# A gradient along rows: unequal shares of the first load among the DMA engines, returned in the last store

## The chip, the cores and the metric

The kernel runs on one core of one Trainium2 chip. The metric is the device time of one execution in microseconds (us), the median of several runs. The engines that matter here are VectorE (DVE), GpSimd (POOL), SyncE (SP), whose queue issues the DMAs, and the sixteen DMA engines behind the queues.

## The reference

```python
x = np.random.randn(8192, 8192).astype(np.float32)

def reference(x):
    return np.gradient(x, axis=1)
```

For each row, `out[j] = (x[j+1] - x[j-1]) / 2` inside, `out[0] = x[1] - x[0]` and `out[m-1] = x[m-1] - x[m-2]` at the two ends. 268 MB are read and 268 MB written.

## The kernel before, in words

The 8192 rows of 8192 columns are cut into `nsets = 32` tiles of 256 rows. Each of the 128 partitions holds `R = 2` whole neighbouring rows, 64 KB in one piece, both in the DRAM and in the on-chip memory; a tile is 8.39 MB. There are `NB = 3` slots; a slot is 64 columns wider than the tile (`SH`), so that the result, which is written over the input 64 columns further left, never overtakes what is still to be read.

For tile `i` the steps are:

- `load(i)`, line 60: one DMA on SP's queue into slot `i % 3`. From tile 3 on it waits for the store that used the slot before.
- Line 70, POOL: the four end differences per partition, kept in the tile `ends`. It waits for the load.
- Line 76, DVE: one custom operation that computes half the difference for all of the two rows. It waits for line 70.
- Line 87, a copy of `ends` into the four end columns, on POOL for some tiles, on DVE for the others (for the last two tiles on DVE).
- Line 89: one DMA on SP's queue that stores the tile. It waits for line 87.

SP's order is written out by hand: loads 0, 1, 2; stores 0, 1, 2; loads 3, 4, 5; stores 3, 4, 5; and so on to stores 27, 28, 29; loads 30, 31; stores 30, 31. An SP instruction that waits holds up those behind it. `chain` declares which earlier steps an instruction needs, and replaces the dependencies that would be found automatically.

Of the kernel before, what the change touches and what calls it, by code (L numbers as in the profile page):

```python
# [1 line left out]

# [4 lines left out]


@with_exitstack
def kernel(  # L10
    ctx: ExitStack,
    tc: tile.TileContext,
    x: bass.AP,
    out: bass.AP,
):

    nc = tc.nc
    P = nc.NUM_PARTITIONS
    n, m = x.shape
    R = 2
    NB = 3  # L30
    SH = 64
    W = R * m
    nsets = n // (P * R)
    f32 = x.dtype

    x_sets = x.rearrange("(s p t) m -> s p (t m)", p=P, t=R)
    out_sets = out.rearrange("(s p t) m -> s p (t m)", p=P, t=R)

    pool = ctx.enter_context(tc.tile_pool(name="pool", bufs=1))
    slots = [pool.tile([P, SH + W], f32, name=f"slot{k}", tag=f"slot{k}") for k in range(NB)]  # L40
    ends = pool.tile([P, nsets, R, 2], f32, name="ends", tag="ends")
    loads, stores = [], [None] * nsets
    in_front = {}

    def chain(i, ins, *needed):

        group, engine = f"slot{i % NB}", ins.ins.engine
        keep = [o.ins for o in needed]  # L50
        if in_front.get(engine, (None,))[0] == group:
            keep.append(in_front[engine][1])
        tc.declare_no_dep(ins.ins, group=group, keep=keep, reason="implied by the needed step")
        tc.add_to_no_dep_group(group, ins.ins)
        in_front[engine] = group, ins.ins
        return ins

    def load(i):
        b = slots[i % NB]
        ins = nc.sync.dma_start(out=b[:, SH : SH + W], in_=x_sets[i])  # L60
        loads.append(chain(i, ins, *([stores[i - NB]] if i >= NB else [])))

    with tc.manual_schedule():
        for i in range(NB):
            load(i)
        for i in range(nsets):
            b = slots[i % NB]
            xin = b[:, SH : SH + W].rearrange("p (t m) -> p t m", m=m)

            ins = nc.gpsimd.tensor_sub(  # L70
                out=ends[:, i, :, :],
                in0=xin[:, :, 1 : m : m - 2],
                in1=xin[:, :, 0 : m - 1 : m - 2],
            )
            at = [chain(i, ins, loads[i])]
            ins = nc.vector._custom_dve(  # L76
                dve_ops.TENSOR_TENSOR_REDUCE_SUB_MAX,
                out=b[:, 1 : W - 1],
                in0=b[:, SH + 2 : SH + W],
                in1=b[:, SH : SH + W - 2],  # L80
                s0=0.0,
                s1=0.5,
            )
            halved = chain(i, ins, *at)
            res = b[:, 0:W].rearrange("p (t m) -> p t m", m=m)
            placer = nc.gpsimd if i % 5 in (1, 3) and i < nsets - 2 else nc.vector
            ins = placer.tensor_copy(out=res[:, :, 0 : m : m - 1], in_=ends[:, i, :, :])  # L87
            placed = chain(i, ins, halved)
            ins = nc.sync.dma_start(out=out_sets[i], in_=b[:, 0:W])
            stores[i] = chain(i, ins, placed)  # L90
            if i % NB == NB - 1:
                for k in range(i + 1, min(i + 1 + NB, nsets)):
                    load(k)


# [1 line left out]
_INS = ['x']  # L97
_OUTS = [((8192, 8192), 'float32')]


# [23 lines left out]
```

## Time and profile before

| | |
|---|---|
| median of three runs | 1248.04 us (1247.85 to 1248.38) |
| the profiled execution: span from the first to the last instruction | 1245.7 us |
| DVE busy | 554.6 us, 45% |
| POOL busy | 8.8 us, 1% |
| DMA queue q1 (SP's): share of sixteen engines' span | 99.8% |
| mean rate | 431 GB/s |
| line 76, one operation | 17.22 us |
| load, issue to landing (median) | 58.0 us |
| store, issue to landing (median) | 40.4 us |

The profiled execution has no device time of its own beside its span; the span is set against the median, and the 2.3 us between them are what lies around the span. Busy times are of compute instructions alone; a DMA shows as its issue on an engine's queue, and by its packets. The profile's page gives the packets in sum, and the trace has a record of each: start, duration, size and queue, but not the DMA engine that moved it. "Idle before, releaser" in the rows of an instruction is what its engine waited for last.

### The profile page before, as it was taken

What the parts mean: (1) busy time and instruction counts of PE and PEld (TensorE: products, weight loads), DVE (VectorE), ACT (ScalarE), POOL (GpSimd) and SP (SyncE); (2) the same over time, 40 slices, a digit from 0 to 9 for tenths busy, and PEclk for the clock granted to TensorE, in tenths of its full rate; (3) what the DMA queues carried; (4) which work ended last, traced back from release to release, by engine and by line L of the source; (5) the groups of instructions that cost most, each with busy time, mean ns of one, the idle gap of its engine ahead of it and who ended that gap; (6) DMA issues with size and microseconds to landing.
All of it is one profiled execution on the core that took longest, in us unless ns stands there. A gap on an engine that the chain in (4) does not pass through costs nothing.

```text
span 1245.7 us, 237 instructions
## 1 busy us (share of the span) xinstructions
DVE 554.6 (45%) x52; POOL 8.8 (1%) x48
## 2 busy tenths in 40 slices
DVE  2850583069009702850582079009603840591083
POOL 0000000000000000000000000000000000000000
DMA  9999999999999999999999999999999999999999
GB/s 404 438 436 423 427 431 438 438 438 436 436 427 431 425 438 436 425 434 436 429 434 436 434 436 434 436 434 438 419 436 436 434 438 438 431 434 429 429 410 404
DMA packets 9217, 536.88 MB, mean 431 GB/s; under 512 B 1024, under 2 KB 1024, under 8 KB 1024
## 3 DMA queue, kind: packets, MB, share of 16 engines
q1 hardware_dynamic: 9216, 536.88, 99.8%
q14 instruction: 1, 0.01, 0.0%
HBM read 268.44 MB, written 268.44 MB: 431 GB/s over the span
## 4 chain that ended last, share of the span: by engine, by line
another core or an unknown queue 74%; DVE 18%; DMA 3%; issue 2%; POOL 1%; SPq 0%; POOLq 0%
DVE slot L76 18%; DMA slot<-in_x_dram 3%; POOL ends L70 0%; POOL slot L87 0%; SPq L60 0%; POOLq L119 0%; DVE slot L87 0%
## 5 line engine op out<-in xcount | busy, mean ns | idle before, releaser
L76 DVE CUSTOM_DVE_ANT_0 slot<-slot 128x16382 f32<-128x16382 f32 x32 | 551.2, 17224 | 668.7 <-POOL ends L70 668.7
L70 POOL TENSOR_TENSOR ends<-slot 128x4 f32<-128x4 f32 x32 | 6.3, 198 | 989.6 <-DMA slot<-in_x_dram 989.6
L87 POOL COPY slot<-ends 128x4 f32<-128x4 f32 x12 | 2.3, 190 | 207.9 <-DVE slot L76 207.9
L87 DVE COPY slot<-ends 128x4 f32<-128x4 f32 x20 | 3.4, 172 | 0.7
L108 POOL MEMSET const-bfloat16-1.0<- 128x1 bf16 x1 | 0.1, 101 | 0.0
L108 POOL MEMSET const-uint8-127<- 128x1 uint8 x1 | 0.1, 101 | 0.0
L108 POOL MEMSET const-float32-0.0<- 128x1 f32 x1 | 0.1, 98 | 0.2 <-issue 0.2
L108 POOL MEMSET const-float32-1.0<- 128x1 f32 x1 | 0.1, 98 | 0.0
## 6 DMA issues: line engine op xcount, KB each, us to landing
slot<-in_x_dram SPq DMA_DIRECT2D x32, 58.0
out_dram<-slot SPq DMA_DIRECT2D x32, 40.4
```

The lines of the kernel that those rows point to most:

```text
L70: ins = nc.gpsimd.tensor_sub(out=ends[:, i, :, :], in0=xin[:, :, 1 : m : m - 2], in1=xin[:, :, 0 : m - 1 : m - 2],)
L76: ins = nc.vector._custom_dve(dve_ops.TENSOR_TENSOR_REDUCE_SUB_MAX, out=b[:, 1 : W - 1], in0=b[:, SH + 2 : SH + W], in1=b[:, SH : SH + W - 2],
L87: ins = placer.tensor_copy(out=res[:, :, 0 : m : m - 1], in_=ends[:, i, :, :])
L108: nc = _bacc.Bacc("TRN2", target_bir_lowering=False, num_devices=1)
```

## The change

The first load and the last store are each cut into several DMAs; everything between is as before.

- The first load becomes four DMAs on SP's queue: columns 0 to 6143 of both rows of partitions 112 to 127; partitions 0 to 111 whole; and the remaining 2048 columns of both rows, once for 12 partitions (112 to 123) and once for 4 (124 to 127). Line 70 of tile 0 waits for all four.
- The last store is cut the same way, but its last columns go out as four DMAs of 4 partitions each on Pool's queue; the two large parts stay on SP's.
- Two small loads on Pool's queue (64 columns of both rows of a few partitions, into a tile `turns` that nothing reads) are added: one of 4 partitions after the first three loads, and one of 12 partitions between the third and the fourth of the small stores.

```diff
+    EVEN, CUT = P - 16, m - 2048
+
+    def parts_of(dram, i, sb, last):
+        whole = dram.rearrange("(s p t) m -> s p t m", p=P, t=R)[i]
+        rows = sb.rearrange("p (t m) -> p t m", m=m)
+        cuts = [(slice(EVEN, P), slice(0, CUT))]
+        first = EVEN
+        for k in last:
+            cuts.append((slice(first, first + k), slice(CUT, m)))
+            first += k
+        pairs = [(whole[p, :, c], rows[p, :, c]) for p, c in cuts]
+        pairs.insert(1, (dram.rearrange("(s p t) m -> s p (t m)", p=P, t=R)[i][0:EVEN], sb[0:EVEN]))
+        return pairs
...
+    turns = pool.tile([16, R, 64], f32, name="turns", tag="turns")
...
     def load(i):
-        b = slots[i % NB]
-        ins = nc.sync.dma_start(out=b[:, SH : SH + W], in_=x_sets[i])
-        loads.append(chain(i, ins, *([stores[i - NB]] if i >= NB else [])))
+        sb = slots[i % NB][:, SH : SH + W]
+        after = [stores[i - NB]] if i >= NB else []
+        parts = parts_of(x, i, sb, (12, 4)) if i == 0 else [(x_sets[i], sb)]
+        loads.append(
+            [chain(i, nc.sync.dma_start(out=to, in_=of), *after) for of, to in parts]
+        )
+
+    def pass_by(first, k):
+        rows = x.rearrange("(p t) m -> p t m", t=R)[first : first + k, :, 0:64]
+        nc.gpsimd.dma_start(out=turns[first : first + k], in_=rows)
...
         for i in range(NB):
             load(i)
+        pass_by(0, 4)
...
-            at = [chain(i, ins, loads[i])]
+            at = [chain(i, ins, *loads[i])]
...
+            if i == nsets - 1:
+                parts = parts_of(out, i, b[:, 0:W], (4, 4, 4, 4))
+                for k, (to, of) in enumerate(parts):
+                    queue = nc.sync if k < 2 else nc.gpsimd
+                    chain(i, queue.dma_start(out=to, in_=of), placed)
+                    if k == 4:
+                        pass_by(4, 12)
+                continue
             ins = nc.sync.dma_start(out=out_sets[i], in_=b[:, 0:W])
             stores[i] = chain(i, ins, placed)
```

## The prediction

> **What bounds the kernel now.** I read the page first, the engine rows beside the DMA rows.
>
> ```profile
> span 1245.7 us, 237 instructions
> DVE 554.6 (45%) x52; POOL 8.8 (1%) x48
> ...
> DMA packets 9217, 536.88 MB, mean 431 GB/s; under 512 B 1024, under 2 KB 1024, under 8 KB 1024
> ...
> q1 hardware_dynamic: 9216, 536.88, 99.8%
> ...
> slot<-in_x_dram SPq DMA_DIRECT2D x32, 58.0
> out_dram<-slot SPq DMA_DIRECT2D x32, 40.4
> ```
>
> VectorE works 45% of the span; the one DMA queue works 99.8% of it. 64 transfers of 8.39 MB made 8192 large packets and 1024 tiny ones: per transfer 128 rows of 64 KB and 16 end marks, so each transfer runs on sixteen DMA engines, eight rows on each. All bytes at 431 GB/s take 1245.7 us. No compute edit matters; what matters is bytes per engine, and time in which an engine has none. Next, the windows near the end (start:end, length, DVE and POOL busy, clock, DMA share, GB/s):
>
> ```profile
> 1200.00:1202.00 2.00, 2.00 (x1) 0.00 (x0) 1.00 1.06 459
> 1202.00:1204.00 2.00, 2.00 (x1) 0.00 (x0) 1.00 0.46 197
> 1204.00:1206.00 2.00, 0.56 (x2) 0.00 (x0) 1.00 1.23 524
> ```
>
> These put a packet in one slice, so they swing by a packet's length, but the dip to 0.46 is real. The timeline says why:
>
> ```profile
> 1186.93 0.20 POOL L70 TENSOR_TENSOR ends<-slot 128x4 f32<-128x4 f32 x1 [77.07 <-DMA slot<-in_x_dram]
> 1187.17 17.22 DVE L76 CUSTOM_DVE_ANT_0 slot<-slot 128x16382 f32<-128x16382 f32 x1 [59.84 <-POOL ends L70]
> ...
> 1204.62 19.69 SPq L89 DMA_DIRECT2D out_dram<-slot  x2
> 1206.28 0.20 POOL L70 TENSOR_TENSOR ends<-slot 128x4 f32<-128x4 f32 x1 [19.14 <-DMA slot<-in_x_dram]
> ...
> 1223.77 0.17 DVE L87 COPY slot<-ends 128x4 f32<-128x4 f32 x1
> ```
>
> Load 30 has landed on all engines at 1186.93, and store 30 is issued 17.69 us later, at 1204.62. Until then an engine has only load 31. The trace's packet records (start and length of each packet; I joined each to the one that starts where it ends, which gives sixteen engines) show the rest: a 64 KB packet takes 2.42 us; before store 30 the slowest engine is 2.3 us behind the fastest, and four engines lie 2.1 to 2.3 behind. The fastest finish load 31 near 1202.4 and stand idle until store 30's first packet at 1204.9; the slowest finishes at 1205.26. From there all have two stores, 16 packets, 38.7 us, and end between 1243.7 and 1243.9. So the end is set by when the slowest engine finishes load 30, then 19.5 us until store 30's first packet, then 38.7 us, then 1.8 us until the span ends. The profiled execution's 1245.7 us stands 2.3 below the median of 1248.04; I take that difference as unchanged and add my sum to the median.
>
> **The change, part by part.**
>
> *First load in four transfers.* It issues three more on SP, 0.42 us each (the rows of the first three issues: 0.38, 0.42, 0.42). The first, 16 partitions by 2 rows by 24 KB, is 0.79 MB and 1.8 us at 431 GB/s, so the next is queued before it ends: nothing on the path. Loads 1 and 2 are issued 1.3 us later behind 19 us of queued work: nothing. Without that queue the price would be 1.3 us. L70 of tile 0 waits for four transfers; on Pool nothing else is due before tile 1, store 0 is issued at 40.40 while its turn in the queue comes after load 2 lands (L70 at 62.44), so 20 us hide any delay there. More descriptors (24 KB and 8 KB instead of 64 KB) have no row; from 0 to 0.1 us, taken as 0.
>
> *Shares.* The last 2048 columns of 16 partitions, 256 KB, an even 16 KB per engine, move as 12 and 4 partitions. If a partition's two rows stay on one engine, four engines have two such pieces, eight one and four none: +16 KB, 0 and −16 KB. 16 KB on an engine is 262144 B over sixteen at 431 GB/s, 0.61 us. So from the first tile on, four engines run 0.61 us late and four 0.61 early, up to the last store. What that does to load 30 depends on which engine is slowest: between −0.61 (all four late ones in the early group; the fifth is 0.8 us ahead of them) and +0.61 (the slowest of all in the late group). The records name no engines; with four late engines of sixteen, one in the group that gets more is likely. I take +0.4. The Trainium skill, "DMA: Bandwidth & Descriptors", section "Why a DMA increments its semaphore by 16 and not by 1", says that such a transfer takes the lowest-numbered engines, so that 0 to 3 would be late and 12 to 15 early; no row here shows engine numbers, and the first load's packets starting one after another over 0.69 us is only a hint at an order.
>
> *Last store.* 16 partitions by 24 KB and the other 112 go out on SP; the 256 KB go as four transfers of 4 partitions on Pool's queue, with a small load of 12 partitions before the fourth. If Pool's queue takes the sixteen engines in turn, one for each partition, the first tile's small load uses the first four, three of the stores the next twelve, the load of 12 the first twelve again, and the fourth store the last four: 0, 16 and 32 KB. Those that had 16 KB less now have 16 KB more, and per engine the bytes of the whole run are even. But the time is not: all engines but the slowest start store 30 together at 1204.9, so the early group's head start has been spent waiting, and its 16 KB more end 0.61 us after the others. Against the slowest engine of before, which ended about 0.2 after most, that is +0.4. The late group ends 0.61 earlier, which helps nobody.
>
> *Pool's issues.* No row shows a DMA issued on Pool. The nearest is SP's issue, 0.34 us: five are 1.7 us after 1223.97, beside store 31's 19.4 us. They reach the end only if one takes more than about 3.5 us (five in 17.5). The first small load stands before L70 of tile 0 on Pool, which waits 22.27 us there. Bounds 0 and +1 (completion seen later, a second queue mixed in); I take +0.1, near the SP row. A page speaks against it: the same page, "Rules for kernel authors", calls transfers under 64 KB mostly overhead, and its fit of 2.0 us for each would make five 10 us, 8 more than the row, still inside store 31 and so 0 by either.
>
> *Switches from loads to stores.* Here the change can pay. The records show the packet at such a switch lengthened: at the first (57.4 us) all sixteen took 3.16 to 3.82 us, 1.1 more than 2.42; at the nine later ones the mean extra was 0.18, 0.07, 0.41, 0.62, 0.15, 0.12, 0.35, 0.00 and 0.06 us, and the slowest engine lost 2.6 in all. Spread among the engines was 0.6 us at the first switch, 2.0 by the fifth, 2.4 in the last, cheap ones. So a spread made on purpose might be cheaper from the start; but the two dearest later switches came at spreads of 1.25 and 1.8, which the change would pass through, and in them the late engines lost most (that feeds the lag). Bounds −2.6 (all later losses gone) and +1; I take −0.3, as the rows point both ways.
>
> *Sum:* 0.4 + 0.4 + 0.1 − 0.3 = +0.6 us: 1248.6. 0.2% is 2.5 us, about what a measurement of this kernel can tell from no change; the sum is well inside.
>
> **The rivals.**
>
> *Shares misplaced (slower).* The last store's four small transfers go to the same engines each time, or to those that were late. Place: the last 19 us. Four pieces on one group are 64 KB, 48 KB over even: 1.8 us on the end. With 0.6 from the first tile if those are the late ones, the extra 0.1, and 0.4 if the lag feeds itself at the switches, +2.9: 1250.9. It decides 0.2% from about 66 KB of surplus, or its time, on the last engine. For it: Pool's placing is not in this trace, and the two helper loads only matter if a rotating turn exists. Against: counted in turns of sixteen, the sizes 4, 4, 4, 4, 12, 4 end where they began, on the right four, whatever the order of speeds.
>
> *Staggered switches (faster).* The switch losses mostly vanish: −2.6 for the later ones, up to −1.0 for the first, +0.8 for shares as above or −0.2 if load 30 comes earlier by the full 0.61: −1.8 to −3.8, so 1244.2 to 1246.2. For it: the cheap late switches at wide spread. Against: the 0.62 at 1.8 us of spread, and the first switch's loss is also the first writing at all.
>
> *Nothing happens.* If the hardware spreads 12 and 4 partitions evenly, or the lagging engines are in the middle and the tail hides the rest, 1248.0 to 1248.2.
>
> **How the numbers follow.** Forecast 0.45, misplaced 0.27 (0.25 of it over 1250.5), staggered switches 0.20 (0.13 of it below 1245.5), nothing 0.08. The likeliest case alone spans −1.5 to +2.0, 1246.5 to 1250.0. To hold 8 in 10 I go to 1245.4 and 1251.2. Faster 0.13, within 0.2% 0.62 (0.45, 0.08, and the 0.09 that the two other cases leave inside), slower 0.25.
>
> **What would show it.** In the packet records, after tile 0 engines in groups 0.6 us apart; the L70 of tile 30 at 1186.9 plus or minus 0.6, store 30 issued 17.7 us behind it. Some engines' last packets 0.6 us behind the rest, Pool's small packets all gone before 1235. Wrong would be: tile 30's L70 more than 1.5 us early (switches cheaper than I took), Pool's packets among the last, a span end more than 1.8 us behind the last large packet, or one engine with four small pieces.

## The result, and the profile after

The changed kernel takes 1281.74 us (median of four, 1280.38 to 1282.05) against 1248.21 for the kernel before beside it: ratio 1.0267, interval 1.0254 to 1.0281, 33.5 us slower. The profiled execution's span is 1278.4 us against 1245.7. The page of the changed kernel, header, row 2, row 3 and the DMA issues (KB each, median us from issue to landing):

```profile
span 1278.4 us, 255 instructions
...
DMA  9999999999999999999999999999999999999997
GB/s 219 338 437 443 429 429 433 441 433 429 437 435 437 424 433 431 439 437 431 429 439 437 431 433 435 433 437 429 427 445 433 431 431 437 437 433 433 433 379 250
DMA packets 9585, 536.89 MB, mean 420 GB/s; under 512 B 1280, under 2 KB 1296, under 8 KB 1296
...
slot<-in_x_dram SPq DMA_DIRECT2D x1, 768.0 KB, 10.1
out_dram<-slot SPq DMA_DIRECT2D x1, 768.0 KB
...
out_dram<-slot POOLq DMA_DIRECT2D x4, 64.0 KB, 25.3
```

The same row of the kernel before:

```profile
GB/s 404 438 436 423 427 431 438 438 438 436 436 427 431 425 438 436 425 434 436 429 434 436 434 436 434 436 434 438 419 436 436 434 438 438 431 434 429 429 410 404
```

The bytes are the same to 0.01 MB, but the rate falls at both ends, in the first two and the last two of 40 slices, just where transfers were cut. Row 2's DMA share reads 9 in the first three of these slices all the same, and 7 in the last: the DMA engines are busy, but their packets are slow. The windows of the changed kernel (start:end, length, DVE and POOL busy, clock, DMA share, GB/s) show a number that came up in several later runs:

```profile
0.00:10.00 10.00, 0.00 (x0) 0.92 (x5) 1.00 1.15 184
10.00:20.00 10.00, 0.00 (x0) 0.00 (x0) 1.00 0.94 210
20.00:30.00 10.00, 0.00 (x0) 0.00 (x0) 1.00 0.73 216
30.00:40.00 10.00, 0.00 (x0) 0.00 (x0) 1.00 1.12 248
40.00:50.00 10.00, 3.97 (x1) 0.20 (x1) 1.00 0.95 348
50.00:60.00 10.00, 10.00 (x1) 0.00 (x0) 1.00 1.00 433
```

An undisturbed window of the kernel before:

```profile
30.00:40.00 10.00, 10.00 (x1) 0.00 (x0) 1.00 0.97 419
```

210 GB/s is half of 419. These figures are coarse: a window counts a packet where it starts, sixteen packets of 64 KB are 1.05 MB, and so 419, 210 and 105 GB/s in 10 us are four, two and one rounds of them. The lengths of the packets say it more finely: 2.42 us on each of sixteen engines is 434 GB/s. The timelines place the loss; first the row of tile 0 before, then the rows of the changed kernel for tiles 0, 30 and 31:

```profile
22.71 0.20 POOL L70 TENSOR_TENSOR ends<-slot 128x4 f32<-128x4 f32 x1 [22.27 <-DMA slot<-in_x_dram]
```

```profile
45.80 0.20 POOL L81 TENSOR_TENSOR ends<-slot 128x4 f32<-128x4 f32 x1 [43.66 <-DMA slot<-in_x_dram]
...
1206.79 0.20 POOL L81 TENSOR_TENSOR ends<-slot 128x4 f32<-128x4 f32 x1 [77.03 <-DMA slot<-in_x_dram]
...
1224.48 0.34 SPq L108 DMA_DIRECT2D out_dram<-slot  x1
...
1244.10 1.73 POOL L104 DMA_DIRECT2D out_dram<-slot  x3 [17.77 <-DVE slot L98]
```

Tile 0's end differences (line 81 now) start at 45.80 instead of 22.71, 23.1 us late. In the packet records the 24 KB packets of the 16 partitions last from 2.3 to 9.3, 7.1 us for 0.79 MB, and those of the 112 partitions from 7.5 to 42.1, 34.6 us for 7.34 MB, which is 212 GB/s; at 434 GB/s they would take 1.8 and 16.9. Tile 30's start 19.9 late, so 3.2 came back on the way. From there the span ends 71.7 us later, before 58.7: 12.9 more. 19.9 + 12.9 is the 32.8 us between the spans. Store 30 is still issued 17.69 us behind tile 30's start, so that step stands.

### The profile page after: what moved, and what is told of

It is laid out like the page before. It is cut to its first block, busy times and chain, and to the rows that moved or that the text cites. A ratio compares the mean times of both kernels' runs of the same rounds, so it can differ in the third digit from the quotient of the medians.

```text
span 1278.4 us, 255 instructions
## 1 busy us (share of the span) xinstructions
DVE 554.6 (43%) x52; POOL 12.5 (1%) x54
## 4 chain that ended last, share of the span: by engine, by line
another core or an unknown queue 75%; DVE 18%; DMA 3%; POOL 1%; issue 0%; SPq 0%; POOLq 0%
DVE slot L87 18%; DMA slot<-in_x_dram 3%; POOL ends L81 1%; POOL slot L98 0%; SPq L66 0%; POOL out_dram L104 0%; POOL turns L71 0%; POOLq L138 0%; DVE slot L98 0%; POOLq L81 0%
## 5 line engine op out<-in xcount | busy, mean ns | idle before, releaser
L81 POOL TENSOR_TENSOR ends<-slot 128x4 f32<-128x4 f32 x32 | 6.4, 200 | 1007.6 <-DMA slot<-in_x_dram 1007.6
## 6 DMA issues: line engine op xcount, KB each, us to landing
slot<-in_x_dram SPq DMA_DIRECT2D x1, 768.0 KB, 10.1
out_dram<-slot POOLq DMA_DIRECT2D x4, 64.0 KB, 25.3
```

Source lines behind the costliest of these rows:

```text
L81: ins = nc.gpsimd.tensor_sub(out=ends[:, i, :, :], in0=xin[:, :, 1 : m : m - 2], in1=xin[:, :, 0 : m - 1 : m - 2],)
```

## The experiments

Of each edit only the lines that matter are shown. The first three runs are edits of the changed kernel, all others of the kernel before; where a `return` line is shown, it stands in a helper whose pieces replace the one transfer of load 0, and in the two runs by columns that of the last store too.

The ports theory, a supposition at this point: DMA engines reach the on-chip memory through ports that belong to certain partitions; a transfer on 128 partitions keeps sixteen engines on different ports, one on 112 or 16 puts several engines on one port at a time, and they share it. Its rivals: small pieces are slow (descriptors); Pool's queue disturbs SP's; few partitions or few engines per transfer cost; the DRAM addresses do.

**One half of the change at a time.** `load_only` leaves out the cut store and the small loads:

```diff
-        pass_by(0, 4)
...
-            if i == nsets - 1:
+            if False:
```

> Only the first load is cut as in the change; the last store is one transfer, nothing is on Pool's queue. The changed kernel's profile has tile 0's L81 23.1 us later than before (45.80 against 22.71) and tile 30's 19.9 later. Ports theory (a transfer of 112 or 16 partitions has several DMA engines at the same port of the on-chip memory) and descriptor theory (24 KB and 8 KB pieces are slow): both expect this half alone to carry about 20 us, 1266 to 1270. Pool theory (the second queue with its small load disturbs the first tile too): under 5 us, below 1253.

Measured: 1268.99 us beside 1248.40, ratio 1.0165 (1.015 to 1.018), 20.6 us slower. Tile 0 is 23.4 us late without anything on Pool's queue, so Pool is not why the first load is slow.

`store_on_sp` leaves the first load whole and puts the last store's six pieces on SP:

```diff
-        parts = parts_of(x, i, sb, (12, 4)) if i == 0 else [(x_sets[i], sb)]
+        parts = parts_of(x, i, sb, (12, 4)) if False else [(x_sets[i], sb)]
...
-        pass_by(0, 4)
...
-                    queue = nc.sync if k < 2 else nc.gpsimd
+                    queue = nc.sync
-                    if k == 4:
-                        pass_by(4, 12)
```

> Only the last store is cut, into the same six pieces, but all on SP's queue, and the two small loads are gone. The changed kernel's profile puts 12.9 us behind tile 30's L81. Ports theory: the 112 partitions and the 16 partitions cost by themselves, so 9 to 13 us stay, 1257 to 1261. Pool theory: the second queue is what slows the last store, so under 3 us are left, below 1251. Descriptor theory: as ports theory here.

`store_with_pool` leaves only the first load whole:

```diff
-        parts = parts_of(x, i, sb, (12, 4)) if i == 0 else [(x_sets[i], sb)]
+        parts = parts_of(x, i, sb, (12, 4)) if False else [(x_sets[i], sb)]
```

> The last store and the two small loads as in the change, the first load whole. Ports theory: within 1.5 us of the run with all pieces on SP, and with the run that cuts only the load the two excesses add up to the change's 33.5 us within 2 us. Pool theory: 8 us or more above the run with all pieces on SP.

Measured: on SP 1262.68, ratio 1.0117 (1.0102 to 1.0132), 14.3 us slower; with Pool 1262.00, ratio 1.0111 (1.0094 to 1.0128), 13.6. Pool's queue adds nothing that these runs can tell. 20.6 and 13.6 make 34.2, against 33.5 for the change. The expectation of 9 to 13 us for the run on SP was a little low. Its windows in the last store:

```profile
1220.00:1225.00 5.00, 4.71 (x2) 0.00 (x0) 1.00 0.97 419
1225.00:1230.00 5.00, 0.00 (x0) 0.00 (x0) 1.00 1.20 123
1230.00:1235.00 5.00, 0.00 (x0) 0.00 (x0) 1.00 0.92 244
1235.00:1240.00 5.00, 0.00 (x0) 0.00 (x0) 1.00 0.95 341
1240.00:1245.00 5.00, 0.00 (x0) 0.00 (x0) 1.00 0.86 341
```

The 16 partitions go first: in the packet records their 24 KB packets take 3.5 to 4.6 us, where the two runs by columns below show 0.91. The 112 partitions then run at 322 GB/s over their whole transfer, better than the 212 of the load.

**Small pieces on all partitions.** `columns_128` cuts the first load and the last store by columns:

```diff
+        return [(whole[:, :, c], rows[:, :, c]) for c in (slice(0, 6144), slice(6144, m))]
```

> First load and last store are each cut into two transfers by columns, 6144 and 2048, on all 128 partitions, on SP's queue: 256 pieces of 24 KB and 256 of 8 KB each, more small pieces than the change has, but sixteen engines on 128 partitions in every transfer. Ports theory: within 1.5 us of before, 1247 to 1249.5. Descriptor theory: at least what the change costs, over 1275; if only the number of pieces counts, several times that.

Measured: 1252.69, ratio 1.0035 (1.0022 to 1.0048), 4.3 us slower: neither expectation. The waits of SP's queue name the reason:

```profile
SPq L68 <- DMA slot<-in_x_dram: 16.7, 1, 16.7
```

The second column transfer waited for the first, presumably since the two stretches interleave within a partition and are taken for overlapping; in the packet records no engine had anything from 17.7 to 19.5, and each stood still for 2.1 us on average. `columns_4` removes what is thought to make it wait, by four transfers of one stretch each:

```diff
+        at = (0, 6144, m, m + 6144, W)
+        return [(whole[:, c:d], sb[:, c:d]) for c, d in zip(at, at[1:])]
```

> As the cut by columns on 128 partitions, but in four transfers that each touch one stretch of a partition (24, 8, 24 and 8 KB), since in the run before the second column transfer waited 16.7 us on SP for the first, and the DMA engines stood still for 2.3 us after it. Ports theory: that wait was most of the 4.3 us; without it 1 to 2 us over before (248 small pieces in the profile cost 5 to 7 ns each over their share, and the first packet starts later), 1248.5 to 1250.5. Descriptor theory: 4 us or more again.

Measured: 1248.06 beside 1247.89, ratio 1.0005 (0.9995 to 1.0014), no difference, and a little less than was expected; that wait is gone from its trace. 512 pieces of 24 and of 8 KB cost nothing that is seen; in the packet records of `columns_128` they take 912 and 309 ns, 5 and 7 over their share of a 64 KB packet. Descriptor theory is out, and so is the number of transfers: four in a row cost nothing.

**Which partitions.** `rows_112_16` cuts the first load into 112 and 16 partitions of whole rows:

```diff
+        return [(whole[p], sb[p]) for p in (slice(0, 112), slice(112, P))]
```

> Only the first load is cut, into partitions 0 to 111 and 112 to 127, whole 64 KB rows, no small piece and no transfer on fewer than sixteen engines. Ports theory: nearly the whole loss of the run that cuts only the load, 15 to 20 us. Descriptor theory: under 2 us. A theory that blames the transfers on 12 and on 4 engines: under 2 us.

Measured: 1267.92, ratio 1.0162 (1.0142 to 1.0182), 20.0 us, as much as the whole cut load. So neither the small pieces nor the transfers on 12 and 4 partitions carry more than about 1 us of it.

`16s_contiguous` and `16s_spread` make eight transfers of 16 partitions each, from the same DRAM addresses into neighbouring or spread partitions:

```diff
+        return [(whole[p], sb[p]) for p in ([slice(16 * j, 16 * j + 16) for j in range(8)])]
```

> The first load is cut into eight transfers of 16 neighbouring partitions, 64 KB each, on sixteen engines. The changed kernel's 24 KB packets on 16 partitions took up to 3.65 us, four times 0.91, so four engines seem to share what one gets otherwise. Ports theory: every packet about 9.7 us, eight of them 77 us instead of 19, tile 0's L70 some 58 us later and the time near 1300 to 1306. Theory of few partitions per transfer or of DRAM addresses: the same as its sister run with spread partitions. The Trainium skill's SBUF page, section on the DMA port swizzle, gives four ports for 16 neighbouring partitions; by it the 58 us follow.

```diff
+        return [(whole[16 * j : 16 * j + 16], sb[j:P:8]) for j in range(8)]
```

> The same eight transfers from the same DRAM addresses, but the 16 partitions of each lie 8 apart (j, j+8, ..., j+120). The rows of tile 0 so stand in other partitions, and its output rows are in another order. Ports theory: the partitions reach twice as many ports, two engines share each, packets about 4.8 us, tile 0's L70 some 19 us later, 1264 to 1269. DRAM or few-partitions theory: as with neighbouring partitions, within 3 us of it.

Measured: 1301.84, ratio 1.0434 (1.0413 to 1.0455), 54.0 us slower, and 1268.54, ratio 1.0167 (1.0147 to 1.0187), 20.7 slower. Windows of the neighbouring ones, then of the spread ones:

```profile
40.00:50.00 10.00, 0.00 (x0) 0.00 (x0) 1.00 0.93 105
50.00:60.00 10.00, 0.00 (x0) 0.00 (x0) 1.00 0.93 105
```

```profile
10.00:20.00 10.00, 0.00 (x0) 0.00 (x0) 1.00 1.02 210
20.00:30.00 10.00, 0.00 (x0) 0.00 (x0) 1.00 1.00 210
```

A quarter and a half of 419, and packets of 9.3 and 5.1 us against 2.42, which over sixteen engines is 113 and 206 GB/s against 434. The transfers have the same number, size and DRAM addresses; only the partitions differ. That decides for the memory's side against DRAM and against few rows per transfer.

`halves_64` is the simplest cut, two halves:

```diff
+        return [(whole[p], sb[p]) for p in (slice(0, 64), slice(64, P))]
```

> The first load in two transfers of 64 neighbouring partitions, 64 KB rows, sixteen engines, four partitions each: the simplest cut there is. The runs so far gave 105 GB/s for 16 neighbouring partitions and 210 for 16 spread ones and for most of the 112. Ports theory: 64 neighbours reach half of the ports, 210 GB/s, 40 us instead of 19.4, tile 0 about 20 us later, 1266 to 1270. A theory that only counts per engine that are no power of two (7 of 112) or only few rows per engine (1) cost: within 2 us of before.

Measured: 1268.54, ratio 1.0167 (1.0149 to 1.0186), 20.7 us slower, its load at half the rate from the start, with packets of 5.1 us:

```profile
10.00:20.00 10.00, 0.00 (x0) 0.00 (x0) 1.00 1.02 210
20.00:30.00 10.00, 0.00 (x0) 0.00 (x0) 1.00 1.01 210
```

**Stores.** `store_16s` cuts the last store into eight transfers of 16 neighbouring partitions:

```diff
+            if i == nsets - 1:
+                for j in range(0, P, 16):
+                    ins = nc.sync.dma_start(out=out_sets[i][j : j + 16], in_=b[j : j + 16, 0:W])
+                    chain(i, ins, placed)
+                continue
```

> The last store in eight transfers of 16 neighbouring partitions, whole 64 KB rows, the first load whole. It asks whether reading the on-chip memory meets the same ports. If it does just as writing: 105 GB/s, 77 us instead of 19.4, some 54 to 58 us slower, 1302 to 1306. If stores suffer less, as the 13 to 14 us of the cut last store against 20 of the cut first load suggest: 20 to 40 us.

Measured: 1284.03, ratio 1.0291 (1.0273 to 1.031), 36.1 us: reading meets the same limit, but loses less than the 54 of the load. Its windows:

```profile
1230.00:1240.00 10.00, 0.00 (x0) 0.00 (x0) 1.00 0.87 105
1240.00:1250.00 10.00, 0.00 (x0) 0.00 (x0) 1.00 0.77 164
1250.00:1260.00 10.00, 0.00 (x0) 0.00 (x0) 1.00 1.13 269
1260.00:1270.00 10.00, 0.00 (x0) 0.00 (x0) 1.00 0.50 111
```

It begins at a quarter, with all sixteen packets of the first transfer at 9.8 to 10.0 us. From the third on, packets take between 2.42 and 8.4 us. A reading that fits is that some engines get ahead into the next transfer's partitions, where they are alone, and the rate rises, until the laggards are left at the end; the records name no engines, so it is not shown. In the load of neighbouring 16s all packets of the later transfers took 9.3 and nobody got ahead. Why these stores share unevenly and these loads evenly stays open. No run cuts the last store into 112 and 16 whole rows; that its loss in the changed kernel is of the same kind rests on this run and on the long 24 KB packets of `store_on_sp`.

**Spread on purpose, without a cut.** `stagger_8_4` puts two small loads ahead of load 0; `stagger_8` only the first of them:

```diff
+    early = pool.tile([16, 2048], f32, name="early", tag="early")
...
+        nc.sync.dma_start(out=early[0:8], in_=x[0:8, 0:2048])
+        nc.sync.dma_start(out=early[8:12], in_=x[8:12, 0:2048])
         for i in range(NB):
             load(i)
```

> No transfer of the kernel is cut; two small loads into a tile nothing reads stand ahead of load 0 on SP (8 partitions and 4 partitions of 8 KB), which should hold the engines they run on back by 1.2 us each, so that engines pass from loads to stores at different times. In the changed kernel tile 30's L70 was 3.2 us less late than tile 0's, so switches cost less there. If spread is the reason: up to 3.2 gained, 1.2 to 2.4 paid, 1245.5 to 1248. If not: 1248.5 to 1250.5, the delay alone.

> Only the first of these two small loads, 8 partitions of 8 KB. If spread is what makes the switches cheap: 1245.5 to 1247.5. If not: 1248.3 to 1249.5, some 0.6 to 1.2 us of delay.

Measured: 1249.30, ratio 1.0011 (1.0002 to 1.002), and 1248.23, ratio 1.0005 (0.9996 to 1.0014). The two loads delay tile 0 by 1.7 us and tile 30 by 1.9; nothing comes back. The one load delays them by 0.4 and 0.4. The 8 KB packets took 0.3 to 0.6 us, not the 1.2 that was expected. By the end marks of load 2, the spread among the engines at the first switch was 0.6 us before, 0.7 in `stagger_8`, which so tests little, and 2.0 in `stagger_8_4`. No version of these beats the kernel before.

## Why the prediction was wrong

**The step that failed** is the first one, "First load in four transfers": "The first, 16 partitions by 2 rows by 24 KB, is 0.79 MB and 1.8 us at 431 GB/s". The 431 GB/s come from transfers on 128 partitions and were used for other shapes. The packets of this transfer took 7.1 us (10.1 from issue to landing on the page), and the 112 partitions, which the prediction did not price at all, ran at 212 GB/s, 34.6 us instead of 16.9. In place of "nothing on the path" stands 23.1 us at tile 0. The "20 us" that "hide any delay there" hid none of it: the queue itself was held up, and tile 2's load too came 21.7 us late (L81 at 84.16, L70 before at 62.44). The last store failed in the same way: "+0.4" stands against 13.6 in the run that cuts only it. No term and no bound allowed a transfer a lower rate than 431 GB/s, so the range could not reach the result.

The Trainium skill, "SBUF — State Buffer", section "Door 1: The DMA port swizzle (why `[64,N]` ≈ `[32,N]`)", says that a DMA's rate depends on how many of sixteen ports its partitions reach, and lists the partitions of each. By its table 16 neighbouring partitions reach four ports, and 64 neighbours, or 16 that lie 8 apart, reach eight; the runs agree, with 113, 205 and 206 GB/s by the length of their packets. This page spoke against the change, and the prediction did not weigh it. An estimate from its table, if each engine has seven neighbouring partitions, which no record shows, gives 22 us for the 112 partitions; in `rows_112_16` they took 34.7 us (packets from 1.8 to 36.5, fifteen of the sixteen end marks at 31.4 to 33.7). So that shape, which carries most of the loss at tile 0, is worse than this estimate. Shown is that the partitions set the rate for 16 and 64 of them, and that a load of 112 runs at half; why the 112 do stays open.

**Pool's issues:** "+0.1" was not contradicted, with 1262.00 against 1262.68 without Pool's queue; runs that differ by a microsecond cannot tell it from nothing. But "Pool's small packets all gone before 1235" was wrong in kind: the small stores took 25.3 us (median) from issue to landing beside SP's queue, and Pool's last landed 0.4 us after the last large transfer; the span ended 2.4 us behind the last large packet, where more than 1.8 was named as a sign of being wrong. They cost little only because the 112 partitions were as late. Pool's issue took 0.58 us, SP's row said 0.34.

**Shares:** the trace agrees that transfers of 12 and 4 partitions run on fewer engines, with 12 and 4 end marks for them instead of 16. The 0.61 us per 16 KB could not be read beside 23.

**Switches:** "−0.3" with a bound of −2.6; from tile 0 to tile 30 the changed kernel gained 3.2 us. Some 1.4 of that came by tile 2, and every run whose first load was stretched to about twice its time or more gained 1.2 to 1.4 there. The packet records show most of it at the first switch: in these six runs no packet there is longer than 2.45 us, and in the eight others all sixteen are lengthened, by 1.0 to 1.2 us on average. Spread does not decide it: it was 0.4 us in `halves_64`, without that loss, and 2.0 in `stagger_8_4`, with it. What does is open. The other 1.9 us are not shown to be more than chance: two runs that are the same up to the last store, but for one small load, were 0.8 us later than before at tile 30. The staggered runs gained nothing.

**Readings of the packet records:** the prediction's packet times near the end stand 0.6 us early against the timeline: store 30's first packet is at 1205.5, not 1204.9, and the span ends 1.2 us behind the last packet, not 1.8. The slowest engine was 3.0 us behind the fastest by the end marks of load 30, not 2.3. Nothing of the 33.5 us hangs on this.

**The rivals:** the slower one, misplaced shares, had the right sign by another mechanism, which is luck, and its 1250.9 missed by 31 us. The faster one expected up to −1.0 at the first switch, and that loss did go, but not through spread. A rival that asked for the rate of a transfer on fewer than 128 partitions was missing.

## What to carry to other kernels

Where a DMA-bound kernel moves whole 128-partition tiles, a cut along the partitions changes the rate and not only the number of transfers: a load in two halves of 64 took as long as two whole tiles. Cut along the columns, with each transfer in one stretch of a partition, and the cut was free here, at 24 and 8 KB a piece. And a rate read from the profile holds for the shape of transfer that made it; for another shape ask which memory partitions the engines touch at the same time.

## What the runs showed of the hardware that was not expected

- Loads by the length of their packets: 434 GB/s on 128 partitions, 205 on 64 neighbouring ones, 206 on 16 that lie 8 apart, 113 on 16 neighbouring ones, all on sixteen engines with 64 KB rows.
- Busy DMA engines say nothing of this: the busy share was 9 tenths and more at half the rate. The GB/s row and the packet lengths show it.
- Transfers of 16 neighbouring partitions shared the rate evenly as loads (9.3 us for every packet from the second transfer on), as stores they did not (2.42 to 8.4 us from the third transfer on).
- Four 64 KB stores on Pool's queue beside a busy SP queue took 25.3 us (median) to land.
- The first switch from loads to stores lengthened all sixteen packets by 1.0 to 1.2 us on average in eight runs, and none in the six whose first load was stretched.
